# Filter network on 128 rows of half the times, projection weights loaded right behind x, filter tables and decay by GpSimd's queue, and idle transposes at the start

## The chip, the cores and the metric

The kernel runs on one core of one Trainium2 chip. The metric is the device time of one execution, in microseconds (us). Of the kernel before, three runs gave 1152.41, 1156.58 and 1158.32, so its median is 1156.58 us. All rows shown of it come from one more execution, which the hardware profiler recorded.

## The reference

The kernel computes one encoder layer on x of 1024 positions by 1024 channels in float32. Cut to what matters here:

```python
h = rms_norm(x, g_norm)
proj = h @ w_in                      # 1024 x 5280: hyena input, gates, latent q and kv, ...
# implicit filters of the long convolution, L = 1024 positions
z = concat([t, cos(ang), -sin(ang)])         # (L, 33), a constant table
f = sin(freq_1 * (z @ w_f1 + b_f1))          # (L, 64)
f = sin(freq_2 * (f @ w_f2 + b_f2))          # (L, 64)
k = (f @ w_f3).reshape(L, 2, 2, 512) * decay # order, direction, channel
k_spec = rfft(concat([k[:, :, 0], k[::-1, :, 1]]))   # filter spectra
u = short_conv(proj[...]); v, x1, x2 = split(u)
for o, gate in enumerate((x1, x2)):
    v = gate * (irfft(rfft(v, 2 * L) * k_spec[:, o])[:L] + v * hy_bias[o])
# beside it: latent attention of 8 heads; both branches are gated, merged, and w_out adds to x
```

## The kernel before, in words

A float32 product is made of three matmuls: each operand is split into a high part that ScalarE casts and a low part that VectorE subtracts (`split`, `gsplit`, `mm3`). The tiles are 128 partitions wide. A scheduler puts the instructions of each engine into one fixed order before the run, and each engine works through its own list in order. DMAs are issued from lists too: SP's and ScalarE's in this kernel; a DMA behind a waiting instruction on its list waits with it. Buffers come from pools; a tile in memory that another tile held waits until the last reader of that one is done.

The start runs like this. Eight tiles of x (`x`, 512 KB each) are loaded by SP and ScalarE in turn (`load_x`), and behind them on SP `sel`, `wf1`, `wf2`, the position table `z2` (`filter_loads`) and the first projection weights `wr` (`proj_block`, L559). `build_hT` works in two halves of four x tiles: squares with sums (ScalarE L216, VectorE L214), twelve small VectorE instructions that make the reciprocal root (`rsqrt`, L152 to L158), scaled rows `xs` (L223), transposes into PSUM (`ptx`, L230), and the split into `hh` (L142) and `hl` (L143). From these the projection is computed block by block: `proj_block` loads two `wr` of 256 KB, makes `wh` and `wl` of each, and issues 48 matmuls `pm` of 128x512 (L567). The first blocks are eight of the gates (`fill_g`); their results go out as `gT`.

The filter network (`filter_mlp`) has both directions of time on 128 partitions, the direction's 64 hidden rows above each other, and all 1024 positions in two chunks of 512. So each of its two layers has two chunks with three matmuls `pf`, a sine layer (VectorE L254 to L260 brings the argument into range, ScalarE L261 takes the sine) and a split. `filter_tables` loads `w_f3` and splits it into `w3h` and `w3l`, and loads the transform tables `ku` as `kur` and splits them into `kuh` and `kul`. `filter_spectra` then makes four spectra (two orders, two halves of the channels): per spectrum four `dec` tables of 512 KB by SP's queue (L342), matmuls `pk` (L348, L349), products `kk` (L350), sums `A` and `B`, small transforms on VectorE (`w`, `res`, `rh`, `rl`), matmuls `pu` with `kuh` and `kul` (L128), and copies `kt` that go to DRAM as `kd`.

Behind the spectra come the projection blocks for the convolution (`proj_vx`: transposes `ptt`, copies `tt`, DMAs `u` and `x`), the tables of the second transform (`load_gu`: DMAs `gur` on SP's list, L621, then `guh` and `gul`), and the convolutions themselves (`convs`): `U` is read back from DRAM, its transforms meet the spectra `kt`, and matmuls `pu` and `pi` with `guh` and `gul` follow. `gur` and `U` share the tag `UY` of the pool `uq`, which lies in memory that the filter's pool `fp` has given back. The rest (attention, output products) is the same text before and after.

## Time and profile before

| | before |
|---|---|
| median of three runs | 1156.58 us (1152.41 to 1158.32) |
| profiled execution | 1155.32 us, span 1153.4 us |
| TensorE (PE) busy | 1099.4 us, 95% of the span, 5525 matmuls |
| VectorE (DVE) busy | 893.0 us, 77% |
| ScalarE (ACT) busy | 589.4 us, 51% |
| GpSimd (POOL) busy | 107.3 us, 9%, no DMA |
| DMA | 150.27 MB, mean 130 GB/s |

Busy time is the sum over instructions of an engine; the matmuls' ends are modelled. PEclk in a table by windows is the clock that TensorE was granted, 1.00 for 2.4 GHz and 0.50 for 1.2 GHz. In a timeline a row gives the start, the duration, the engine (SPq and ACTq are the lists that issue DMAs), the source line, and in brackets how long the engine stood idle before it and what released it. "L12" is line 12 of the kernel before in every row below; in the kernel after, lines stand 7 to 16 further down.

### The profile page before, as it was taken

What the parts mean: (1) busy time and instruction counts of PE and PEld (TensorE: products, weight loads), DVE (VectorE), ACT (ScalarE), POOL (GpSimd) and SP (SyncE); (2) the same over time, 40 slices, a digit from 0 to 9 for tenths busy, and PEclk for the clock granted to TensorE, in tenths of its full rate; (3) what the DMA queues carried; (4) which work ended last, traced back from release to release, by engine and by line L of the source; (5) the groups of instructions that cost most, each with busy time, mean ns of one, the idle gap of its engine ahead of it and who ended that gap; (6) DMA issues with size and microseconds to landing.
All of it is one profiled execution on the core that took longest, in us unless ns stands there. A gap on an engine that the chain in (4) does not pass through costs nothing.

```text
span 1153.4 us, 15529 instructions
## 1 busy us (share of the span) xinstructions
PE 1099.4 (95%) x5525; PEld 909.7 (79%) x5525; DVE 893.0 (77%) x1631; ACT 589.4 (51%) x1101; POOL 107.3 (9%) x112
## 2 busy tenths in 40 slices
PE   4899999999999999999999999999999999999996
PEld 3678888888888888878887887787888887778874
DVE  6988788698788886778774893789788888478882
ACT  6745555754445434433433852777877776322420
POOL 0000000000000000000000132102200000250353
PEclk9989999999999999999999999899999999999998
DMA  5446444642335334334227557402202001896345
GB/s 212 133 146 198 155 163 174 205 119 65 89 91 147 105 115 128 91 88 127 91 83 233 148 154 248 146 29 74 92 25 77 1 20 50 274 298 217 91 128 182
DMA packets 119221, 150.27 MB, mean 130 GB/s; under 512 B 8548, under 2 KB 82408, under 8 KB 119144
## 3 DMA queue, kind: packets, MB, share of 16 engines
q1 hardware_dynamic: 107688, 120.97, 34.1%
q10 hardware_dynamic: 11456, 28.32, 6.6%
q8 instruction: 43, 0.70, 0.3%
q14 instruction: 34, 0.28, 0.1%
HBM read 101.81 MB, written 47.45 MB: 129 GB/s over the span
## 4 chain that ended last, share of the span: by engine, by line
PE 65%; DVE 14%; DMA 10%; ACT 6%; issue 3%; POOL 1%; SPq 0%; ACTq 0%; POOLq 0%; DVEq 0%
PE pm L567 33%; PE pu L128 8%; PE pt L903 4%; PE pi L128 4%; DMA wor<-in_w_out_dram 3%; PE S L119 2%; PE S L122 2%; PE S L121 2%; ACT pr L889 2%; PE pv L915 2%; PE pv L916 2%; DVE gg L988 1%; DMA out_dram<-xr 1%; DVE mo L139 1%; ACT PTh L138 1%
## 5 line engine op out<-in xcount | busy, mean ns | idle before, releaser
L567 PE MATMUL pm<-hh,wh 128*128 128x512 f32 x656 | 208.6, 393 | 1.8 <-DVE hl L143 0.9
L567 PE MATMUL pm<-hl,wh 128*128 128x512 f32 x656 | 208.9, 393 | 0.0
L567 PE MATMUL pm<-hh,wl 128*128 128x512 f32 x656 | 208.3, 392 | 0.1
L567 PEld LDWEIGHTS pm<-hh,wh 128*128 128x128 f32 x656 | 123.1, 189 | 27.7 <-DVE hl L143 1.1
L567 PEld LDWEIGHTS pm<-hh,wl 128*128 128x128 f32 x656 | 123.2, 188 | 26.0 <-DVE wl L139 0.5
L567 PEld LDWEIGHTS pm<-hl,wh 128*128 128x128 f32 x656 | 123.0, 188 | 25.3
L138 ACT CAST wh<-wr 128x512 fp32r<-128x512 f32 x98 | 60.3, 621 | 158.1 <-PE pm L567 107.7
L138 ACT CAST PTh<-pt 128x512 fp32r<-128x512 f32 x128 | 72.8, 587 | 41.1 <-PE pt L903 39.6
L139 DVE TENSOR_TENSOR PTl<-pt,PTh 128x512 fp32r<-128x512 f32 x128 | 83.8, 682 | 10.8 <-ACT PTh L138 10.2
L887 DVE TENSOR_REDUCE mx<-S 128x1 f32<-128x1024 f32 x64 | 77.9, 1217 | 13.2 <-PE S L122 13.1
L139 DVE TENSOR_TENSOR wl<-wr,wh 128x512 fp32r<-128x512 f32 x95 | 66.8, 708 | 15.7 <-ACT wh L138 15.4
L903 PE MATMUL pt<-ident,pr 128*128 128x128 f32 x512 | 75.9, 278 | 2.4 <-DVE PTl L139 1.4
L889 ACT ACTIVATE pr<-S,mx 128x1024 f32<-128x1024 f32 x64 | 71.8, 1121 | 7.0 <-DVE mx L887 6.6
L903 PEld LDWEIGHTS pt<-ident,pr 128*128 128x128 f32 x512 | 59.3, 142 | 18.2 <-DVE PTl L139 4.7
L915 PE MATMUL pv<-PTh,vc 128*128 128x256 f32 x256 | 69.1, 297 | 0.4 <-DVE at L926 0.4
L916 PE MATMUL pv<-PTl,vc 128*128 128x256 f32 x256 | 67.9, 293 | 0.0
L473 DVE TENSOR_TENSOR t<-pu,kt 128x512 f32<-128x512 f32 x64 | 41.0, 681 | 31.3 <-PE pu L128 30.7
L138 ACT CAST rh<-res 128x512 fp32r<-128x512 f32 x64 | 39.5, 619 | 41.8 <-PE pu L128 20.5
L119 PE MATMUL S<-kh,qh 96*128 96x512 f32 x128 | 54.5, 426 | 2.4 <-ACT pr L889 2.3
L121 PE MATMUL S<-kh,ql 96*128 96x512 f32 x128 | 53.5, 418 | 0.0
L122 PE MATMUL S<-kl,qh 96*128 96x512 f32 x128 | 52.5, 410 | 0.0
L915 PEld LDWEIGHTS pv<-PTh,vc 128*128 128x128 f32 x256 | 48.5, 189 | 4.7 <-DVE at L926 1.9
(285 smaller groups left out, 2391.2 us busy)
## 6 DMA issues: line engine op xcount, KB each, us to landing
wr<-in_w_in_dram SPq DMA_DIRECT2D x82, 256.0 KB, 3.2
wor<-in_w_out_dram SPq DMA_DIRECT2D x36, 256.0 KB, 4.7
dec<-in_dec_dram SPq DMA_DIRECT2D x16, 512.0 KB, 3.6
gT<-ob ACTq DMA_DIRECT2D x16, 512.0 KB, 2.9
gg<-gT SPq DMA_DIRECT2D x16, 512.0 KB, 4.4
kd<-kt ACTq DMA_DIRECT2D x28, 256.0 KB, 2.3
kt<-kd SPq DMA_DIRECT2D x28, 256.0 KB, 2.7
m<-gg ACTq DMA_DIRECT2D x16, 256.0 KB, 4.3
```

The lines of the kernel that those rows point to most:

```text
L119: m = nc.tensor.matmul(out, lhsT=lh, rhs=rh, start=start, stop=False)
L121: nc.tensor.matmul(out, lhsT=ll, rhs=rh, start=False, stop=False)
L122: nc.tensor.matmul(out, lhsT=lh, rhs=rl, start=False, stop=stop)
L128: m = self.nc.tensor.matmul(out, lhsT=x, rhs=y, start=n == 0, stop=n == len(ops) - 1)
L138: self.behind(self.nc.scalar.copy(out=hi, in_=x), after)
L139: (eng or self.nc.vector).tensor_tensor(out=lo, in0=x, in1=hi.bitcast(F32), op=ALU.subtract)
L567: nc.tensor.matmul(ps[c][0:m], lhsT=w[:, i, 0:m], rhs=h[d][:, c * 512:(c + 1) * 512], start=(d == 0 and f == 0), stop=(d == 7 and f == 2))
L887: nc.vector.tensor_reduce(out=mx, in_=ps, axis=AX.X, op=ALU.max, negate=True)
L889: i = nc.scalar.activation(out=pr, in_=ps, func=AF.Exp, bias=mx, accum_out=RS[h // 2][:, qb, h % 2:h % 2 + 1])
L903: nc.tensor.transpose(out=pt[:, i], in_=pr[:, kb * P:(kb + 1) * P], identity=self.ident)
L915: nc.tensor.matmul(pv, lhsT=V[h][:, kb], rhs=hi[:, kb], start=(kb == 0), stop=False)
L916: nc.tensor.matmul(pv, lhsT=V[h][:, kb], rhs=lo[:, kb], start=False, stop=(kb == 7))
```

## The change

The filter network now works on the first 512 positions in the upper 64 rows and on the last 512 in the lower 64, for one direction; the other direction is the same result read backwards. One chunk per layer is left, with three `pf` instead of six, and the second direction is made by two reversed casts on VectorE (`h[:, ::-1]`). The high and low parts of `z2` and `ku` come from the host as tables of their own, so no engine splits them. GpSimd issues the DMAs of `z2h` and `z2l` (256 KB each) once the seventh x tile is there, those of `kuh`, `kul` (1.18 MB each) and `sel` once `hh[7]` of the first half is there (`follow`), and all `dec` and `hy_bias` tables. `sel` and `z2` no longer stand before the first `wr` on SP's list. `w_f3` is loaded twice (four DMAs of 256 KB), so that its split needs two instructions of 128 rows per engine instead of half rows. 36 transposes of raw x tiles into a PSUM tile that nothing reads (`idle`) stand on TensorE before the first `ptx`. The gates' output is issued one block later (`gates`), and the second gate block's split is put behind `half0`, the last cast of the first half. The last step of the range reduction in a sine layer merges two constants into one (three L258 become two).

```diff
-    z2 = np.zeros((P, L), f32)
-    z2[:33] = z.T
-    z2[64:97] = z[::-1].T
+    z2 = np.zeros((P, L // 2), f32)
+    z2[:33] = z[:L // 2].T
+    z2[64:97] = z[L // 2:].T
...
+    t = {"sel": sel, "gu": gu, "dec": d2, "rt": rt, "ident": np.eye(P, dtype=f32)}
+    for n, x in (("z2", z2), ("ku", ku)):
+        t[n + "h"], t[n + "l"] = _parts(x)
+    return t
...
+        idle = self.pp.tile([P, 512], F32, tag="tp", bufs=2, name="idle")
+        for i in range(4):
+            for j in range(8 if i < 3 else 12):
+                nc.tensor.transpose(out=idle[:, :P], in_=xt[i][:, (j % 8) * P:(j % 8 + 1) * P], identity=self.ident)
...
-    def filter_loads(self, f1):
+    def filter_loads(self, fp, f1):
         nc, a = self.nc, self.a
-        self.selr = f1.tile([P, P], F32, tag="selr", name="selr")
-        nc.sync.dma_start(out=self.selr, in_=a["sel"])
         self.wf1 = f1.tile([P, P], F32, tag="wf1", name="wf1")
         nc.sync.dma_start(out=self.wf1, in_=a["wf1"])
         self.wf2 = f1.tile([P, P], F32, tag="wf2", name="wf2")
         nc.sync.dma_start(out=self.wf2, in_=a["wf2"])
-        self.z2 = f1.tile([P, L], F32, tag="z2", name="z2")
-        nc.sync.dma_start(out=self.z2, in_=a["z2"])
+        self.z2 = [f1.tile([P, L // 2], F32R, tag="z" + x, name="z" + x) for x in "hl"]
+        self.kuh = fp.tile([P, 18, P], F32R, tag="kuh", name="kuh")
+        self.kul = fp.tile([P, 18, P], F32R, tag="kul", name="kul")
+        self.sel = self.cp.tile([P, P], F32R, tag="sel", name="sel")
+        self.follow(f1, self.xt[6][0:1, 0:1], ((self.z2[0], a["z2h"]), (self.z2[1], a["z2l"])))
+
+    def follow(self, pool, x, moves):
+
+        nc = self.nc
+        dum = pool.tile([1, 1], F32, tag="fol", bufs=2, name=self.nm("fol"))
+        last = nc.gpsimd.tensor_copy(out=dum, in_=x)
+        for out, in_ in moves:
+            i = nc.gpsimd.dma_start(out=out, in_=in_)
+            self.behind(i, last)
+            last = i
 
     def filter_mlp(self, fp, f1):
+
         nc, a = self.nc, self.a
         self.w3h = [fp.tile([P, 2, HY], F32R, tag=f"w3h{d}", name=f"w3h{d}") for d in range(2)]
         self.w3l = [fp.tile([P, 2, HY], F32R, tag=f"w3l{d}", name=f"w3l{d}") for d in range(2)]
-        self.h2 = [fp.tile([P, L], F32R, tag=f"h2{d}", name=f"h2{d}") for d in range(2)]
-        z2, fv = self.z2, self.fv
-        zh = f1.tile([P, L], F32R, tag="zh", name="zh")
-        zl = f1.tile([P, L], F32R, tag="zl", name="zl")
+        self.h2 = {(d, c): fp.tile([P, L // 2], F32R, tag=f"h2{d}{c}", name=f"h2{d}{c}") for d in range(2) for c in range(2)}
+        fv, (zh, zl) = self.fv, self.z2
+        self.follow(f1, self.hh[7][0:1, 0:1].bitcast(F32), ((self.kuh, a["kuh"]), (self.kul, a["kul"]), (self.sel, a["sel"])))
+
+        wf3 = [f1.tile([P, 2, HY], F32, tag=f"wf3{d}", name=f"wf3{d}") for d in range(2)]
+        w3v = a["w_f3"][0].rearrange("k (o d c) -> d k o c", o=2, d=2)
+        for d in range(2):
+            for s in range(2):
+                self.behind(nc.scalar.dma_start(out=wf3[d][64 * s:64 * s + 64], in_=w3v[d]), self.half0)
         w1h = f1.tile([P, P], F32R, tag="w1h", name="w1h")
         w1l = f1.tile([P, P], F32R, tag="w1l", name="w1l")
         w2h = f1.tile([P, P], F32R, tag="w2h", name="w2h")
         w2l = f1.tile([P, P], F32R, tag="w2l", name="w2l")
         self.split(self.wf1, w1h, w1l, after=self.half0)
         self.split(self.wf2, w2h, w2l, after=self.half0)
-        h1h = f1.tile([P, L], F32R, tag="h1h", name="h1h")
-        h1l = f1.tile([P, L], F32R, tag="h1l", name="h1l")
+        h1h = f1.tile([P, L // 2], F32R, tag="zh", name="h1h")
+        h1l = f1.tile([P, L // 2], F32R, tag="zl", name="h1l")
+        ps = self.pp.tile([P, L // 2], F32, tag="cv", bufs=CVB, name=self.nm("pf"))
+        self.mm3(ps, w1h, w1l, zh, zl, True, True)
+        x = self.sin_layer(f1, ps, fv[:, 0:1], fv[:, 1:2], L // 2)
+        self.split(x, h1h, h1l)
+        for d in range(2):
+            self.split(wf3[d], self.w3h[d], self.w3l[d], after=self.half0)
+        ps = self.pp.tile([P, L // 2], F32, tag="cv", bufs=CVB, name=self.nm("pf"))
+        self.mm3(ps, w2h, w2l, h1h, h1l, True, True)
+        x = self.sin_layer(f1, ps, fv[:, 2:3], fv[:, 3:4], L // 2)
         for c in range(2):
...
+            a_, b_ = slice(64 * c, 64 * c + 64), slice(64 - 64 * c, 128 - 64 * c)
+            h, r = self.h2[0, c], self.h2[1, 1 - c]
+            nc.scalar.copy(out=h[a_], in_=x[a_])
+            nc.vector.tensor_tensor(out=h[b_], in0=x[a_], in1=h[a_].bitcast(F32), op=ALU.subtract)
+            nc.vector.tensor_copy(out=r, in_=h[:, ::-1].bitcast(F32))
...
-                nc.sync.dma_start(out=bia, in_=a["hy_bias"][:, o, cs])
+                nc.gpsimd.dma_start(out=bia, in_=a["hy_bias"][:, o, cs])
                 for tp in range(4):
                     dec = wk.tile([P, 2, 2, CW], F32, tag="dec", bufs=2, name=self.nm("dec"))
-                    nc.sync.dma_start(out=dec, in_=a["dec"][hf, tp].rearrange("p (d t c) -> p d t c", d=2, t=2))
+                    nc.gpsimd.dma_start(out=dec, in_=a["dec"][hf, tp].rearrange("p (d t c) -> p d t c", d=2, t=2))
...
+                            b = 2 * tp + i
+                            h = h2[d, b // 4][:, b % 4 * P:(b % 4 + 1) * P]
+                            nc.tensor.matmul(ps[:, i], lhsT=h, rhs=w3h[d][:, o, cs], start=True, stop=False)
+                            nc.tensor.matmul(ps[:, i], lhsT=h, rhs=w3l[d][:, o, cs], start=False, stop=True)
...
-    def proj_block(self, c0, m=P):
+    def proj_block(self, c0, m=P, after=None):
...
-            self.split(raw[:, :, 0:m], wh[:, :, 0:m], wl[:, :, 0:m])
+            self.split(raw[:, :, 0:m], wh[:, :, 0:m], wl[:, :, 0:m], after=after)
...
-    def fill_g(self, b):
+    def gates(self, bs):
+
+        ps = None
+        for b in bs:
+            new = self.proj_block(3232 + b * P, P, self.half0 if b == 1 else None)
+            if ps is not None:
+                self.gate_out(b - 1, ps)
+            ps = new
+        self.gate_out(bs[-1], ps)
+
+    def gate_out(self, b, ps):
         nc = self.nc
-        ps = self.proj_block(3232 + b * P, P)
...
-                with k.pool("fpb") as fb:
-                    k.filter_tables(fb)
-                    with k.pool("fwk") as wk:
-                        k.filter_spectra(wk)
-                        for b in range(GEARLY):
-                            k.fill_g(b)
+                with k.pool("fwk") as wk:
+                    k.filter_spectra(wk)
+                    k.gates(range(GEARLY))
```

Two places show how the order moves. The first is VectorE's list at the start. Before, the first reciprocal root (`rt_176`, `ry_175`) runs through to the scaled rows `xs`, and the low parts `wl` of the first projection weights stand in the second one (`rt_263`, `ry_262`):

```order
L156 TENSOR_TENSOR rt_176<-ry_175 128x4
L157 SCALAR_TENSOR_TENSOR rt_176<-rt_176,rv_174 128x4
L158 SCALAR_TENSOR_TENSOR ry_175<-rt_176,ry_175 128x4
L223 TENSOR_SCALAR xs_189<-x_115,ry_175 128x1024
...
L223 TENSOR_SCALAR xs_195<-x_121,ry_175 128x1024
L152 TENSOR_SCALAR rv_261<-ss 128x4
L153 TENSOR_SCALAR rt_263<-rv_261 128x4
L139 TENSOR_TENSOR wl_1569<-wr_1566,wh_1568 128x512
L154 TENSOR_SCALAR ry_262<-rt_263 128x4
L139 TENSOR_TENSOR wl_1599<-wr_1596,wh_1598 128x512
```

Now both `wl` stand inside the first one (`rt_218`, `ry_217`):

```order
L165 TENSOR_TENSOR rt_218<-ry_217 128x4
L148 TENSOR_TENSOR wl_1558<-wr_1555,wh_1557 128x512
L166 SCALAR_TENSOR_TENSOR rt_218<-rt_218,rv_216 128x4
...
L165 TENSOR_TENSOR rt_218<-ry_217 128x4
L148 TENSOR_TENSOR wl_1588<-wr_1585,wh_1587 128x512
L166 SCALAR_TENSOR_TENSOR rt_218<-rt_218,rv_216 128x4
L167 SCALAR_TENSOR_TENSOR ry_217<-rt_218,ry_217 128x4
L233 TENSOR_SCALAR xs_231<-x_115,ry_217 128x1024
```

So the scaled rows now stand behind two instructions that need the weights `wr_1555` and `wr_1585` and ScalarE's casts of them, and on ScalarE's list the second cast stands behind the square of x tile 4.

The second place is SP's list about the end of the spectra. Before, the two DMAs `gur` of the second transform's tables stand ahead of all four DMAs `u` that carry the first convolution's input to DRAM (the last two come from `tt_2263`); each `gur` waits for a `pk` matmul of the last spectrum, the last reader of the memory that it fills:

```order
L621 DMA gur_2454<-in_gu_dram 128x1408
L621 DMA gur_2458<-in_gu_dram 128x1408
...
L613 DMA u_0_2104<-tt_2177 512x1x128
L613 DMA u_1_2105<-tt_2177 512x1x128
L481 DMA kt_2490<-kd_0_8_571 128x768
L481 DMA kt_2537<-kd_0_12_592 128x512
...
L613 DMA u_0_2104<-tt_2263 512x1x128
L613 DMA u_1_2105<-tt_2263 512x1x128
L559 DMA wr_2956<-in_w_in_dram 128x4x128
L699 DMA U_2462<-u_0_2104 128x1024
L699 DMA U_2462<-u_1_2105 128x1024
```

Now they stand about the last two `u` DMAs (`tt_2251`), and the first of them waits for the last `pu` matmul with `kuh` of the last spectrum:

```order
L566 DMA wr_2386<-in_w_in_dram 128x4x128
L566 DMA wr_2873<-in_w_in_dram 128x4x128
L628 DMA gur_2442<-in_gu_dram 128x1408
L620 DMA u_0_2092<-tt_2251 512x1x128
L620 DMA u_1_2093<-tt_2251 512x1x128
L628 DMA gur_2446<-in_gu_dram 128x1408
L488 DMA kt_2478<-kd_0_8_560 128x768
L488 DMA kt_2525<-kd_0_12_581 128x512
L715 DMA U_2450<-u_0_2092 128x1024
L715 DMA U_2450<-u_1_2093 128x1024
```

So the tables `gur`, which have moved into memory that `kuh` and `kul` held, are asked for later in the work, and the DMAs `u` and `U` of the first convolution stand behind them.

## Rows read from the trace of the kernel before

**Rows 1.** Busy time and granted clock of stretches (start:end, length, busy of each engine; instructions)

```profile
core 0: us, PE busy (x) PEld busy (x) DVE busy (x) ACT busy (x) POOL busy (x), PEclk, DMA share, GB/s
53.00:58.00 5.00, 0.00 (x1) 0.00 (x0) 5.00 (x8) 4.48 (x7) 0.00 (x0) 0.99 0.40 160
58.00:65.00 7.00, 5.68 (x17) 4.67 (x18) 5.64 (x10) 3.80 (x6) 0.00 (x0) 0.52 0.44 140
65.00:83.00 18.00, 18.00 (x92) 15.30 (x91) 15.59 (x28) 5.60 (x10) 0.00 (x0) 1.00 0.57 180
100.00:600.00 500.00, 499.61 (x2345) 412.20 (x2344) 399.88 (x774) 232.86 (x460) 1.60 (x24) 1.00 0.40 124
```

**Rows 2.** Timeline of the start: reciprocal root, scaled rows, transposes, weights, first projection

```profile
12.55 0.17 DVE L152 TENSOR_SCALAR rv<-ss 128x4 f32<-128x4 f32 x1
...
12.89 1.06 ACT L216 ACTIVATE sq<-x 128x1024 f32<-128x1024 f32 x1 [0.36 <-DMA x<-in_x_dram]
...
14.93 2.74 DVE L223 TENSOR_SCALAR xs<-x,ry 128x1024 f32<-128x1024 f32 x4
...
15.74 5.52 PE L230 MATMUL ptx<-ident,xs 128*128 128x128 f32 x28 [8.60 <-DVE xs L223]
...
16.79 0.62 ACT L138 CAST wh<-wr 128x512 fp32r<-128x512 f32 x1 [0.47 <-DMA wr<-in_w_in_dram]
17.57 0.62 ACT L138 CAST wh<-wr 128x512 fp32r<-128x512 f32 x1 [0.16 <-DMA wr<-in_w_in_dram]
...
17.87 0.69 DVE L139 TENSOR_TENSOR wl<-wr,wh 128x512 fp32r<-128x512 f32 x1
...
21.36 4.70 DVE L143 SCALAR_TENSOR_TENSOR hl<-ptx,cols,hh 128x512 fp32r<-128x512 f32 x7 [0.48 <-ACT hh L142]
...
22.17 0.50 PE L567 MATMUL pm<-hh,wh 128*128 128x512 f32 x1 [0.91 <-DVE hl L143]
```

**Rows 3.** Timeline of the filter network and the first spectrum's start

```profile
43.60 1.21 DVE L322 TENSOR_TENSOR w3l<-wf,w3h 64x1024 fp32r<-64x1024 f32 x1
...
51.19 3.69 DVE L258 SCALAR_TENSOR_TENSOR sx<-sk,sx 128x512 f32<-128x512 f32 x6
...
58.86 0.58 PE L348 MATMUL pk<-w3h,h 128*128 128x256 f32 x1 [5.86 <-DVE h L306]
...
83.04 0.28 PE L128 MATMUL pu<-rh,kuh 128*128 128x256 f32 x1
```

**Rows 4.** Chain that ended last, from the spectra's end to the first convolution

```profile
209.81 2.75 PE pu L128 x12
212.56 8.21 PE pm L567 x36
220.76 0.45 PE ptt L611 x4
...
222.47 2.97 DMA u<-tt
...
225.50 5.00 DMA U<-u
...
244.05 1.43 PE pi L128 x12
```

**Rows 5.** The tables `gur` of the second transform (min/median/max in ns, first and last start)

```profile
L138 ACT CAST guh<-gur x2: 1378/1378/1378, 216.9 to 218.2; 128x1408 fp32r<-128x1408 f32 x2
L139 DVE TENSOR_TENSOR gul<-gur,guh x2: 1619/1620/1620, 219.6 to 221.2; 128x1408 fp32r<-128x1408 f32 x2
...
DMA to landing us min/median/max: 4.2/4.2/4.2
```

**Rows 6.** The page's table of DMA issues, the row of `dec`

```profile
dec<-in_dec_dram SPq DMA_DIRECT2D x16, 512.0 KB, 3.6
```

67 lines of the change are left out of this document (14 added, 53 removed).

## The prediction

> **What bounds the kernel now.** I read the table by windows first. From 65 us on TensorE is the bound: 18.00 of 18.00 us busy from 65 to 83, and 499.61 of 500 us from 100 to 600, with VectorE at four fifths [rows 1]. So up to 600 us a microsecond is worth something only where TensorE waits or runs slowly, and that is the start: 0.00 us busy from 53 to 58, and a granted clock of 0.52, the lower of its two levels, in the 7 us behind that idle stretch [rows 1]. Then I read the timeline of the start. The scaled rows `xs` begin at 14.93 us, the first projection matmul at 22.17 [rows 2], the first `pk` comes after 5.86 us of waiting for `h` from the filter network, and the first `pu` stands at 83.04 [rows 3]. Last I read the chain about the first convolution, because the changed order moves its tables [rows 4, 5].
>
> **What TensorE loses at the start.** Between 22.17 and 83.04, 60.9 us, its list holds 171 `pm`, 12 `pf`, 36 transposes and 32 `pk`. A `pm` takes 8.21/36 = 0.228 us, a 128x128 transpose 0.45/4 = 0.113, a 128x256 matmul 1.43/12 = 0.119 [rows 4]. That is 39.0 + 2.7 + 4.1 + 3.8 = 49.6 us, so 11.3 us go to waiting and the lower clock; 5.86 of them are the one wait for `h` [rows 3].
>
> **The change, part by part.**
>
> *Filter on half the times.* Six `pf` go: 6 x 0.228 = 1.4 us of TensorE. On VectorE a sine layer's long steps fall from six in 3.69 us for two chunks [rows 3] to two, some 1.2 us. Two of four sines, the splits of `z2` and `ku` on two engines, and half of the `h` steps go as well. Two reversed casts of 128x512 come in; no row has one, so I bound them by 0.3 us (half of a row below) and 1.4 (twice it) and take the 0.69 us of a `wl` [rows 2]. Shortening this chain pays through the 11.3 us: while it ran, TensorE had only two gate blocks (96 `pm`) ahead of the first `pk`; now its list has 129 there.
>
> *The weights in front.* Both `wl` now stand inside the first reciprocal root, so `xs` waits for two weight loads. Before, the casts of these weights began on landing, at 16.79 and 17.57 [rows 2], 0.78 us for 256 KB. The 512 KB of `z2` and the 64 KB of `sel` that stood ahead would be 1.8 us of that: the first weight lands at 15.0 at the earliest, and at 16.8 if GpSimd's `z2h` and `z2l`, the same bytes, share the engines. I take 16.0. Then come the cast 0.62, `wl` 0.69, six root steps of (14.93 - 12.55)/12 = 0.20 us [rows 2]; on ScalarE the second cast stands behind another square of x, 1.06 us [rows 2], and ends near 18.4. With the second `wl` and two steps `xs` starts at about 19.5, 4.6 us later than now (18.5 to 20.3 by the bounds).
>
> *The idle transposes* do not reach that far. They end soon after the fourth x tile, whose sum is used at 12.55 [rows 2]: 12 last ones at 0.2 are done by 15.0. Up to 20.3 TensorE is idle again for 5 us, as long as the stretch from 53 to 58, behind which the clock was low [rows 1]. So I count `ptx` at today's pace, 28 in 5.52 us [rows 2], and the first `pm` at 22.17 + 4.6 = 26.8. If the clock stays up, 28 x (0.197 - 0.113) = 2.4 us go there, but `hl` then waits for VectorE, and at most 1.3 us arrive.
>
> *New waits between 27 and 65 us.* VectorE's list now has `w1l`, `w2l`, the first range reduction step and two `w3l` (1.21 us each for as many columns [rows 3]) ahead of the second block's `wl`; the third block's load waits for that one. Nothing in the trace shows this wait. It is 1.0 us if the first block's matmuls cover most, and 4.6 if both `w3l` and the load follow one another uncovered. I take 2.8, the middle. `h` should be ready at about 63, which is when TensorE comes to `pk` by its own list (26.8 + 129 x 0.228 + 36 x 0.113 + 1.4 + waits), so the 5.86 us wait is gone, and what is late next is the weights.
>
> *Sum at the first `pu`.* 192 `pm`, 6 `pf`, 36 transposes, 32 `pk` are 53.1 us: 26.8 + 53.1 + 2.8 = 82.7. Before reaches the same work 21 `pm` later than 83.04, at 87.8. TensorE is 5.1 us ahead.
>
> *The tables of the second transform.* Here I expect most of that to be given back. `gur` now waits for the last `pu` of the spectra. Its place: up to it, 11 `pm` and 8 transposes more than before, 3.4 us, so 212.56 [rows 4] + 3.4 + 82.7 - 83.04 = 215.6. The last two `u` and both `U` stand behind it on SP's list. `gur` lands 4.2 us on, `guh` takes 1.4 and `gul` 1.6 [rows 5], then the first `U` may be issued, which takes 5.00 us: 227.8. Before, `U` landed at 230.50 and the first `pi` came at 244.05 [rows 4], 13.55 us later; now that would be 241.4. TensorE's own list holds 92 `pm`, 16 transposes and 12 small `pu` up to that `pi`, 24.2 us (before 31.5), and would be there at 239.8. So it waits 1.6 us at least by this count; 0 if part of those 13.55 us is TensorE's own work; 5.8 if the second `gur` and the two `kt` tables ahead of `U` cost another 4.2 us. I take 3.5.
>
> *`dec` and `hy_bias` by GpSimd.* I cost them at nothing: the first two tables land long before `pk`, and a later one has the time of seven VectorE instructions of 128x512, about 4.8 us, against 3.6 us of landing now [rows 6]. No GpSimd DMA is in this trace, so the landing is open; the bound is the rival below.
>
> **Sum.** 5.1 us ahead at the first `pu` (11.3 lost before and 1.4 of `pf`, against 4.6 and 2.8 of new delay, up to rounding) less 3.5 given back is 1.6: 1155.32 - 1.6 = 1153.7 us by the profiled execution. The median of the runs is 1.3 us above that execution; halfway, I say 1154.3 us. With the bounds (5.1 ahead is 2.5 to 7.5, the later wait 0 to 5.8) this case reaches from 1149 to 1158.5.
>
> **Rivals.**
>
> 1. *The gain is kept.* The weights land at 15.0, or the wait at the first `pi` is hidden, as TensorE has waited only 0.39 us in 500 so far [rows 1]. Then 5 to 7.5 us stay: 1148 to 1150.5. Against it speaks the list of SP, on which nothing can pass `gur`.
> 2. *The shorter network does not reach the end at all.* `xs` at 20.3, waits of 4.6 us, 2.5 ahead, and 3.5 to 5 lost at the tables: 1156 to 1159. For it speaks that one edit puts two DMAs into the root's chain.
> 3. *Slower: `dec` comes late.* If a table by GpSimd's list takes over 4.8 us, `kk` and with it the spectrum wait. At twice today's landing, 7.2 us [rows 6], it is 2.4 us late. The third and fourth table of a spectrum are asked for only once a buffer is free, so 4 x 2 x 2.4 = 19 us over the four spectra; less the 5.1 us ahead that is 1169 with nothing hidden, and with 5 us of it behind gate blocks some 1164. VectorE is busy 15.59 of 18 us there [rows 1], and the lists of GpSimd are otherwise short, so neither is excluded. The Trainium skill, "SBUF — State Buffer", section "SBUF: two separate sides", says that a DMA issued from GpSimd gets its descriptors written by GpSimd itself and starves while VectorE holds the shared port in its fast modes, and gives 3100 instead of 620 ns; by an estimate from these figures 2.5 us would be added, 6.1 in all, which is over the 4.8. Nothing in this trace shows it. The products and sums of the spectra are at the slow pace of 0.69 us for 512 columns, which is why this stays the smallest case.
>
> **How the numbers follow.** The forecast gets 0.53, the first rival 0.23, the second 0.13, the third 0.11. A measurement of this kernel can tell about 0.5%, 5.8 us, from no change: faster is below 1150.8, slower above 1162.4. Faster is the first rival and a little of the forecast, 0.24; slower the third, 0.11; between them 0.65. The range for 8 in 10 takes in the forecast's own range, the upper half of the first rival and the second: 1149 to 1161.
>
> **What would show it.** Right: `xs` at 19 to 20 us, the first `pm` near 27, no wait over 1 us at the first `pk`, the first `pu` near 83 with all of the fourth gate block done, and at about 240 a wait of 2 to 5 us before the first `pi`, with `gur` issued near 216. Wrong: `xs` before 17 (the weights came early), a granted clock of 1.00 and `ptx` at 0.11 us from the first one (the idle transposes hold it), no wait at 240 (then the time is near 1149), or `kk` waiting for `dec` in each spectrum (then it is above 1160).

## The result and the profile after

The changed kernel takes 1163.86 us, the median of 13 runs (1158.56 to 1167.63); the kernel before took 1156.58 us beside it, also of 13 runs (1151.88 to 1160.18). The ratio is 1.0066, with a 95% interval of 1.0051 to 1.0082: slower by 0.66%, 7.6 us, where 1154.3 us was forecast with a range of 1149 to 1161. The profiled execution of after took 1167.63 us (span 1165.8), 12.3 us more than that of before. That is more than the medians differ by, so the accounts below go by how much later TensorE comes to the same matmul than before, and not by the spans.

The table by windows of after, the stretches of [rows 1] and one ahead of them (start:end, length, busy of each engine; instructions):

```profile
core 0: us, PE busy (x) PEld busy (x) DVE busy (x) ACT busy (x) POOL busy (x), PEclk, DMA share, GB/s
45.00:53.00 8.00, 6.05 (x15) 4.62 (x16) 5.51 (x9) 6.12 (x8) 0.00 (x0) 0.57 0.43 124
53.00:58.00 5.00, 5.00 (x23) 4.13 (x22) 1.91 (x3) 2.82 (x5) 0.00 (x0) 1.00 0.49 137
58.00:65.00 7.00, 7.00 (x32) 5.79 (x31) 4.15 (x7) 3.77 (x4) 0.00 (x0) 1.00 0.38 95
...
100.00:600.00 500.00, 496.49 (x2318) 408.19 (x2317) 396.88 (x766) 232.87 (x462) 7.41 (x35) 1.00 0.40 123
```

The idle stretch from 53 to 58 of before is gone, and with it the low clock behind it. But both stand again in front of it: from 45 to 53 TensorE is busy for 6.05 of 8 us at a granted clock of 0.57. From 100 to 600 it now loses 3.5 us, where it lost 0.4.

The start came as forecast. Its timeline in after, beside [rows 2]:

```profile
16.10 0.69 DVE L148 TENSOR_TENSOR wl<-wr,wh 128x512 fp32r<-128x512 f32 x1 [2.54 <-ACT wh L147]
...
18.76 2.74 DVE L233 TENSOR_SCALAR xs<-x,ry 128x1024 f32<-128x1024 f32 x4
...
19.57 6.18 PE L240 MATMUL ptx<-ident,xs 128*128 128x128 f32 x28 [5.84 <-DVE xs L233]
...
26.09 0.50 PE L574 MATMUL pm<-hh,wh 128*128 128x512 f32 x1 [0.34 <-DVE hl L152]
```

VectorE sits 2.54 us in the middle of the reciprocal root, waiting for the first weight and its cast, and `xs` starts 3.83 us later than before.

What went wrong is between 40 and 70 us. Four rows of TensorE's timeline there (columns as in [rows 2]):

```profile
46.95 1.22 PE L574 MATMUL pm<-hh,wh 128*128 128x512 f32 x2 [3.05 <-ACT wh L147]
...
49.67 1.05 PE L574 MATMUL pm<-hh,wh 128*128 128x512 f32 x2
...
53.45 0.62 PE L574 MATMUL pm<-hh,wl 128*128 128x512 f32 x2
...
69.04 0.39 PE L355 MATMUL pk<-w3h,h 128*128 128x256 f32 x1
```

A wait of 3.05 us for a cast, then rows of two `pm` that last 1.05 us where 0.62 is usual, and the first `pk` at 69.04, 10.2 us later than before [rows 3]. TensorE doesn't wait at that `pk`, because gate blocks stand in front of it. ScalarE's timeline shows why `h` is late:

```profile
45.33 1.04 ACT L147 CAST w3h<-wf 128x1024 fp32r<-128x1024 f32 x1 [4.46 <-DMA wf<-in_w_f_dram]
...
51.50 0.62 ACT L147 CAST wh<-wr 128x512 fp32r<-128x512 f32 x1 [1.50 <-DMA wr<-in_w_in_dram]
52.14 1.28 ACT L271 ACT_TABLE_LOAD   x1
53.43 0.63 ACT L271 ACTIVATE sx<-sx 128x512 f32<-128x512 f32 x1
...
61.19 0.62 ACT L147 CAST wh<-wr 128x512 fp32r<-128x512 f32 x1 [4.55 <-PE pm L574]
61.83 1.28 ACT L699 ACT_TABLE_LOAD   x1
63.12 0.69 ACT L699 ACTIVATE ob<-pm,cols 128x512 f32<-128x512 f32 x1
63.83 1.28 ACT L271 ACT_TABLE_LOAD   x1
65.12 0.63 ACT L271 ACTIVATE sx<-sx 128x512 f32<-128x512 f32 x1
65.78 1.28 ACT L699 ACT_TABLE_LOAD   x1
67.07 0.69 ACT L699 ACTIVATE ob<-pm,cols 128x512 f32<-128x512 f32 x1
67.66 0.61 ACT L330 CAST h<-sx 64x512 fp32r<-64x512 f32 x1
```

ScalarE is idle for 4.46 us for the last part of `w_f3`. Then both sines and the casts `h1h` and `h` stand behind casts `wh` that wait for weights still on their way, or for a buffer that TensorE is still reading (4.55), and between gates `ob`, with a table load (`ACT_TABLE_LOAD`, 1.28 us) at each change of function. VectorE has the arguments of the sines ready at 51.30 and 61.86; the sines start at 53.43 and 65.12. VectorE's last step ahead of the second sine:

```profile
61.43 0.43 DVE L270 TENSOR_SCALAR sx<-sx 128x512 f32<-128x512 f32 x1
```

The chain of waits goes the same way (start, length, what; its last row belongs to the second transform, below):

```profile
36.60 8.66 DMA wf<-in_w_f_dram
...
46.95 10.06 PE pm L574 x31
...
222.88 4.81 DMA gur<-in_gu_dram
```

The page's row of `dec`, beside [rows 6], and TensorE's first `pi`:

```profile
dec<-in_dec_dram POOLq DMA_DIRECT2D x16, 512.0 KB, 4.6
```

```profile
248.96 0.39 PE L137 MATMUL pi<-ph,guh 128*128 128x256 f32 x1 [1.28 <-ACT ph L147]
```

`gur`, the tables of the second transform, is issued at 222.88, 7.3 us after the 215.6 of the forecast; 5.1 us of that are the later first `pu`. The first `pi` starts at 248.96 (before 243.9) after a wait of 1.28 us for ScalarE's cast `ph`. `dec` lands in 4.6 us at the median (before 3.6).

### The profile page after: what moved, and what is told of

It reads as the page before. It is cut to its first block, busy times and chain, and to the rows that moved or that the text cites. A ratio compares the mean times of both kernels' runs of the same rounds, so it can differ in the third digit from the quotient of the medians.

```text
span 1165.8 us, 15589 instructions
## 1 busy us (share of the span) xinstructions
PE 1105.7 (95%) x5555; PEld 913.0 (78%) x5555; DVE 882.4 (76%) x1610; ACT 580.0 (50%) x1089; POOL 120.4 (10%) x137
## 4 chain that ended last, share of the span: by engine, by line
PE 63%; DVE 13%; DMA 12%; ACT 7%; issue 3%; POOL 1%; SPq 0%; POOLq 0%; ACTq 0%; DVEq 0%
PE pm L574 29%; PE pu L137 7%; PE pt L919 4%; PE pi L137 4%; DMA wor<-in_w_out_dram 3%; PE S L128 2%; ACT pr L905 2%; PE S L130 2%; PE S L131 2%; PE pv L931 2%; PE pv L932 2%; PE pmo L130 1%; PE pmo L128 1%; DMA out_dram<-xr 1%; PE pmo L131 1%
## 5 line engine op out<-in xcount | busy, mean ns | idle before, releaser
L903 DVE TENSOR_REDUCE mx<-S 128x1 f32<-128x1024 f32 x64 | 77.9, 1217 | 12.8 <-PE S L131 12.6
```

The source lines that it names most:

```text
L903: nc.vector.tensor_reduce(out=mx, in_=ps, axis=AX.X, op=ALU.max, negate=True)
```

## The experiments

The same landmarks of the profiles that the argument uses (us; below zero is ahead of before). "First pu, same work" sets the first `pu` against before's 83.04 and takes off 0.228 us for each `pm` more that stands ahead of it: 171 in before, 192 in after and in `e1`, `e2`, `e9` and `e10`, 168 in `e12` to `e14`, 167 in `e17`. "Behind at 370" is how much later than before TensorE starts the same matmul, at 370 us.

| | ratio to before (95%) | first pk | first pu | first pi | first pu, same work | behind at 370 |
|---|---|---|---|---|---|---|
| before | | 58.9 | 83.0 | 243.9 | 0 | 0 |
| after | 1.0066 (1.0051 to 1.0082) | 69.0 | 87.8 | 249.0 | 0.0 | 5.90 |
| e1_tables_held | 1.0075 (1.0053 to 1.0098) | 69.7 | 88.6 | 250.0 | 0.7 | 5.73 |
| e2_gu_early | 1.0080 (1.0052 to 1.0108) | 68.4 | 87.2 | 252.4 | -0.6 | 8.19 |
| e9_gur_front | 1.0069 (1.0041 to 1.0097) | 67.4 | 86.2 | 247.4 | -1.7 | 10.12 |
| e10_bytes_early | 1.0046 (1.0029 to 1.0063) | 64.6 | 83.4 | 245.7 | -4.4 | 2.60 |
| e14_act_order | 1.0049 (1.0032 to 1.0066) | 62.5 | 81.3 | 248.4 | -1.0 | 4.18 |
| e12_h_early | 1.0002 (0.9991 to 1.0013) | 57.9 | 76.8 | 244.3 | -5.6 | 0.05 |
| e13_h_early_gu | 1.0012 (0.9998 to 1.0025) | 57.9 | 76.8 | 242.2 | -5.6 | -1.82 |
| e17_xs_early | 1.0037 (1.0022 to 1.0053) | 59.7 | 79.4 | 247.3 | -2.7 | 2.85 |

Each landmark is of one execution, and executions of one kernel differ (before: 1151.88 to 1160.18 us). `e16_seven_gates`, which has the start of `e13_h_early_gu`, came to its first `pk` at 60.0 instead of 57.9, so differences of 2 us in these columns say little.

**When the bytes are asked for.** From 20 to 30 us the DMA engines move 21 GB/s in after and from 30 to 40 us 278: GpSimd's `kuh`, `kul` and `sel` (2.4 MB) and `w_f3` (1 MB) run together, and the first two `dec` with them:

```profile
30.00:40.00 10.00, 9.26 (x54) 7.04 (x53) 8.31 (x13) 6.02 (x12) 4.50 (x8) 1.00 0.94 278
```

The first test holds GpSimd's tables until `w_f3` is there:

```diff
-        self.follow(f1, self.hh[7][0:1, 0:1].bitcast(F32), ((self.kuh, ...), (self.kul, ...), (self.sel, ...)))
+        self.follow(f1, wf3[1][64:65, 0, 0:1], ((self.kuh, ...), (self.kul, ...), (self.sel, ...)))
```

> The changed kernel with one edit: GpSimd asks for kuh, kul and sel only when the last w_f3 block has landed. Theory A (the fourth w_f3 block took 8.66 us because the 2.3 MB of tables shared the DMA engines with it, and that is where the gain of the start was lost): w_f3 lands within 4 to 5 us of its issue, near 41 us, no wait of TensorE at 47 us, a granted clock of 1.00 from 45 to 52, the first pu near 83.5 instead of 87.97, and the median 4 to 4.5 us lower, 1159.5. Rival B (the w_f3 block is late by its own queue, ScalarE's): it lands at 45 as now, the first pu stays at 88, the median stays at 1163.9. Rival C (the tables, asked for later, are now what the first pu waits for): w_f3 early, but a wait for kuh before the first pu, and the median within 1 us of 1163.9.

Measured: 1165.35 us, no gain. The wait for `w_f3` is gone (TensorE is busy for 9.09 us of 40 to 50), but the tables now press on the weights. Of its chain, and of its TensorE timeline:

```profile
44.55 7.17 DMA wr<-in_w_in_dram
```

```profile
55.43 0.79 PE L128 MATMUL pf<-h1h,w2h 128*128 128x512 f32 x1 [4.45 <-ACT h1h L147]
```

256 KB of weights take 7.17 us, and the same casts ahead of `h1h` wait for them. Moving the bytes back moved the wait. The second test asks for all of them earlier, in the empty stretch:

```diff
+            self.xs0 = getattr(self, "xs0", xs[0])
...
-        self.follow(f1, self.hh[7][0:1, 0:1].bitcast(F32), (kuh, kul, sel))
...
-                self.behind(nc.scalar.dma_start(out=wf3[d][64 * s:64 * s + 64], in_=w3v[d]), self.half0)
+        self.follow(f1, self.xs0[0:1, 0:1], [(wf3[d][64 * s:64 * s + 64], w3v[d]) ...] + [kuh, kul, sel])
```

> The changed kernel with w_f3 and then kuh, kul and sel asked for by GpSimd behind the first xs, near 19 us, where the DMA engines moved 21 GB/s between 20 and 30 us, instead of behind hh near 30 (the tables) and on ScalarE's list at 36.6 (the fourth w_f3). Theory A (the start is bound by the bytes that are asked for between 30 and 45 us: what is delayed is w_f3 in the changed kernel and the weights wr in e1, so only a shift into the idle stretch helps): no wait of TensorE over 1 us between 30 and 60 us, h at 60 to 62, the first pu near 83.5 instead of 87.97, the median 4 to 4.5 us lower, 1159.5. Rival B (not bytes but ScalarE's and VectorE's lists of the filter network bound the first pk): no DMA wait is left but the first pk still comes after 69, and the median is within 1 us of 1163.9. Rival C (the tables now delay the weights of the second block at 20 to 30 us): a wait for wr or wl before 45 us, gain under 2 us.

Measured: 1162.18 us, and the first `pu` at 83.41, as expected, 4.4 us earlier than in after. The time is not as expected: the ratio is 0.20% lower, 2.3 us, with overlapping intervals. From 20 to 30 us 279 GB/s move, and TensorE's wait of 3.05 us is gone. But ScalarE's list still holds `h` up: a cast `wh` in front of the first sine waits for its load, and one in front of the second for TensorE:

```profile
47.78 0.62 ACT L147 CAST wh<-wr 128x512 fp32r<-128x512 f32 x1 [1.81 <-DMA wr<-in_w_in_dram]
...
56.79 0.62 ACT L147 CAST wh<-wr 128x512 fp32r<-128x512 f32 x1 [4.02 <-PE pm L572]
```

**The order on ScalarE's list.** Now the casts of the third block's weights go behind `h1h`, those of the fourth behind `h`, and the second block's gate behind `h` as well; everything else stays as in the run before:

```diff
-        self.split(x, h1h, h1l)
+        self.h1i = nc.scalar.copy(out=h1h, in_=x)
+        nc.vector.tensor_tensor(out=h1l, ...)
...
-            nc.scalar.copy(out=h[a_], in_=x[a_])
+            self.hi = nc.scalar.copy(out=h[a_], in_=x[a_])
...
-            new = self.proj_block(3232 + b * P, P, self.half0 if b == 1 else None)
+            new = self.proj_block(3232 + b * P, P, {1: self.half0, 2: self.h1i, 3: self.hi}.get(b))
...
+            if b == 1:
+                self.behind(i, self.hi)     # i: the activation that makes ob
```

> e10 with one more edit on ScalarE's list: the casts of the third and fourth block's weights stand behind h1h and h, and the second block's gate behind h, so that neither a wait for wr (45.74 to 51.04 us in e10) nor two extra loads of the activation table (57.43 and 61.37, 1.28 us each) stand ahead of the two sines. Theory A2 (formed from e1 to e11: the four spectra follow each other at 37 to 40 us each at VectorE's pace, so it is the first pk, which waits for h, that sets the last pu and the first pi; 58.9, 212.2 and 243.9 us before the change, 69.0, 222.4 and 249.0 in the changed kernel, 64.6, 218.7 and 245.7 in e10): first pk at 57 to 59, last pu at 212 to 215, first pi at 241 to 244, the median 3 to 5 us under e10's 1162.2, so 1158. Rival B2 (TensorE's own list, not h, sets the end: it is busy all the time from 53 us on in e10, so h can come as early as it likes): first pk early, the first pi not before 245, the median within 1 us of 1162.2.

Measured: 1156.20 us, ratio 1.0002, and 0.6% under the changed kernel: the whole loss is gone, with intervals that lie apart. Of the 11.1 us by which the first `pu` is earlier than in after, 5.5 are 24 `pm` that now stand behind it; 5.6 us are a lead on before in the same work. ScalarE's timeline, to be held against that of after:

```profile
47.62 0.63 ACT L272 ACTIVATE sx<-sx 128x512 f32<-128x512 f32 x1
...
55.83 0.63 ACT L272 ACTIVATE sx<-sx 128x512 f32<-128x512 f32 x1 [4.29 <-DVE sx L271]
56.50 1.26 ACT L329 CAST h<-sx 64x512 fp32r<-64x512 f32 x2
57.78 1.28 ACT L698 ACT_TABLE_LOAD   x1
```

The sine now waits for VectorE's argument, `h` follows it at once, and between the first sine and `h` no table load is left, where three stood. TensorE is busy for 10.00 of 10 us from 45 to 55 and from 55 to 65. The same edit of the order alone, on the changed kernel with its late bytes:

> The changed kernel with the order edit of e12 on ScalarE's list alone; w_f3 and the tables are asked for where the changed kernel asks for them. It tells the two parts of e12 apart. Theory A2 (both parts are needed: the late w_f3 holds the list until 45.3 us, the order costs what comes behind it): w_f3 lands at 45 as in the changed kernel, then one table load, sine, h1h, second sine; h 4 to 6 us earlier than 70.5, first pk at 63 to 65, and the median 3 to 4 us under the changed kernel, 1160. Rival (the order alone is the cause, and the late w_f3 was hidden all along): first pk at 58 to 60 and a median of 1156 to 1157 as in e12. Rival (the transfers alone): first pk at 69, 1163 to 1165.

Measured: 1161.18 us, ratio 1.0049, first `pk` at 62.5. By the ratios the early bytes alone give 0.20% and the order alone 0.17%, and the interval of each overlaps that of after; both together give 0.64%, clear of it. That each obstacle left alone still holds the network up is read from the landmarks: the first `pk` at 64.6 and 62.5, and at 57.9 without both.

**The second transform's tables.** The forecast put its loss at 240 us on `gur`. First the memory is laid out so that `gur` no longer waits for the last `pu` (the weights of the third filter layer are taken ahead of `kuh`):

```diff
+        self.w3h = [...]; self.w3l = [...]; self.h2 = {...}     # moved up, ahead of kuh
         self.kuh = fp.tile([P, 18, P], F32R, tag="kuh", name="kuh")
```

> The changed kernel with one edit: w3h, w3l and h2 are allocated ahead of kuh and kul, so the tables gur of the second transform go into memory whose last reader is the last pk and not the last pu. No instruction changes its place. Theory A (4.4 us between 209 and 273 us were lost because gur had to wait for the last pu): gur is issued near 216 instead of 222.88, no wait over 0.5 us before the first pi, and the median 3.5 to 4.4 us lower, 1160. Rival B (it is the place of gur on SP's list, behind two u and two weight loads, that makes it late): issued at 220 or later, and the median at most 1 us lower.

Measured: 1163.95 us, no gain, and the first `pi` is later, at 252.4. SP's list:

```profile
218.97 0.46 SPq L628 DMA_DIRECT2D gur<-in_gu_dram  x1
222.49 5.71 SPq L620 DMA_DIRECT2D u<-tt  x2
```

`gur` is issued 3.9 us earlier than in after, but the two `u` behind it take until 228.2 to be issued. Then `load_gu` goes ahead of `proj_vx(0)` in the program too, with one weight load behind it:

```diff
-                k.proj_vx(0)
                 k.load_gu(gp)
+                k.proj_vx(0)
...
+            if c0 == 5 * P and g == 1:
+                self.behind(i, self.gur)
```

> The changed kernel with the tables gur of the second transform both in memory whose last reader is the last pk (as in e2) and put ahead of the second pair of u and of the last weight load on SP's list. Theory A (the 4.4 us between 209 and 273 us come from the place of gur in SP's list together with the memory that it waits for): gur issued near 198 us instead of 222.88, VectorE does not wait for gul, the first pi below 247 instead of 248.96, no stretch at the lower clock at 250, TensorE at most 1.5 us behind the kernel before at 273 us instead of 5.0, and the median 3.5 to 4.5 us lower, 1160. Rival B (it is VectorE's own list, which has come later and denser to this place, that sets the first pi; gur only stood in its shadow): gur early, the first pi still after 248, and the median within 1 us of the changed kernel's 1163.9.

Measured: 1164.53 us, ratio 1.0069, as after, although `gur` is issued at 198.0, 25 us earlier. The edit moved more than `gur`: 580 `pm` stand ahead of the first `pi` instead of 608, so TensorE is busy for only 29.7 of the 36 us from 209 to 245 (after 35.0), and the 28 `pm` come back as filler later (153.8 of 160 us busy from 600 to 760, after 147.8). Of the 10.12 us of the table 6.4 are these 28 (at 0.228). VectorE still waits for `guh`, and TensorE for VectorE:

```profile
227.35 1.63 DVE L148 TENSOR_TENSOR gul<-gur,guh 128x1408 fp32r<-128x1408 f32 x1 [7.60 <-ACT guh L147]
```

```profile
244.41 1.53 PE L620 MATMUL ptt<-ident,acc 128*128 128x128 f32 x8 [3.41 <-DVE acc L609]
```

ScalarE casts `guh` at 225.9, where its list has it, not when `gur` lands (4.2 us after its issue). So the transfer was not what ended last there, and the first `pi`, at 247.4, again waits 1.50 us for ScalarE's `ph`. Two more runs join this memory edit to the better starts:

> The edits of e9 and e10 together. Theory A (start and second transform are two separate losses against the gain that the change should have had): 8 us under the changed kernel, a median near 1156, level with the kernel before. Rival B (whatever is saved at one place is waited for at the next, since another engine than TensorE sets the pace up to 273 us): at most 3 us lower, 1161 or more.

> e12 with the memory of e2 (gur waits for the last pk and not for the last pu). In e12 and here gur stands on SP's list ahead of the second pair of u, not behind it as in the changed kernel. Theory A2: with the spectra early there is less filler behind them, so now gur's wait for the last pu shows: gur issued near 195 instead of 213, first pi 1 to 3 us earlier than in e12, median 1156 to 1157. Rival: gur loads beside kd and u and holds them up, as e2 had it (kd 7.29 us), and the time is within 1 us of e12's.

`e11_both` (both edits of `e9_gur_front`, on `e10_bytes_early`) took 1159.85 us, ratio 1.0036 (1.0021 to 1.0050), a little under `e10_bytes_early` though the intervals overlap; `e13_h_early_gu` (`e12_h_early` with the memory of `e2_gu_early`) 1157.47 us, ratio 1.0012, no faster than `e12_h_early`.

**`dec` by GpSimd.** Both DMAs go back to SP's list:

```diff
-                nc.gpsimd.dma_start(out=bia, in_=a["hy_bias"][:, o, cs])
+                nc.sync.dma_start(out=bia, in_=a["hy_bias"][:, o, cs])
...
-                    nc.gpsimd.dma_start(out=dec, in_=a["dec"][hf, tp]...)
+                    nc.sync.dma_start(out=dec, in_=a["dec"][hf, tp]...)
```

> The changed kernel with one edit: dec and hy_bias are asked for by SP's list again, as before the change. Theory A (dec by GpSimd costs next to nothing): the median within 1.5 us of 1163.9. Rival B (dec by GpSimd is late, 4.6 us of landing at the median against 3.6 before, and VectorE waits 3.3 us for it): VectorE's waits for dec gone, TensorE busy 120 of 120 us between 100 and 220 instead of 118.6, and the median 2 to 5 us lower.

Measured: 1165.31 us, ratio 1.0074 (1.0050 to 1.0097), the same as after. VectorE's waits for `dec` fall from 3.3 us to 0.7 without any gain. The landing is the same by either list:

```profile
dec<-in_dec_dram SPq DMA_DIRECT2D x16, 512.0 KB, 4.6
```

So GpSimd's queue is neither the cause of the loss nor of the 1.0 us by which `dec` lands later than before.

**The lead-in to `xs`.** Both `wl` of the first block go behind the first `xs` (`self.behind(wl, xs0)`):

> The changed kernel with one edit: on VectorE both wl of the first projection block stand behind the xs of the first group, as before the change. Theory A (two weight loads inside the root cost 4 us at the start): xs begins near 15 instead of 18.76, the first pm near 22 instead of 26.09, and since the tables are asked for as much earlier, all that follows shifts too: the first pu near 84, the median 4 us lower, 1160. Rival B (the start is bound by bytes: x, weights, w_f3 and tables come through the same DMA engines, and w_f3 lands near 45 whatever xs does): the first pm near 22 but the first pu still near 87 and the median within 1 us of 1163.9. By the way: with 2 us instead of 6 between the idle transposes and ptx the granted clock may stay at 1.00 there; then 28 ptx take about 4 us instead of 6.2.

Measured: 1165.07 us, ratio 1.0084 (1.0059 to 1.0109), no gain. Of its timeline:

```profile
15.87 3.27 PE L241 MATMUL ptx<-ident,xs 128*128 128x128 f32 x28 [1.75 <-DVE xs L233]
...
23.99 0.79 PE L575 MATMUL pm<-hh,wh 128*128 128x512 f32 x1 [4.85 <-DVE hl L152]
```

`xs` and `ptx` are 3.7 us earlier and `ptx` twice as fast, but `hh` stands behind the squares of the second group on ScalarE and begins at 20.80. TensorE waits 4.85 us, has the low clock after that (0.50 from 24 to 28), and the lead of the first `pm` is down to 2.1 us. So on `e13_h_early_gu` the same edit was run with the last two squares moved behind the casts `hh` of the first half:

> e13 with the edit of e4 (both wl of the first block behind the first xs) and, what e4 lacked, the last two squares of the second x group behind the first hh on ScalarE's list (in e4 four squares stood ahead of hh, which began at 20.80 instead of about 18.7, and a second idle stretch of 4.85 us followed). Theory: xs at 15, ptx at a clock of 1.00 in 3.3 us, first pm at 20 to 22 instead of 25.9, first pk at 54 to 56 instead of 57.9, last pu 2 to 4 us earlier than 206.1, first pi 2 to 4 us earlier than 242.2, and the median 2 to 4 us under e13's 1157.5: 1154 to 1155. Rival (the second x group now comes late): a wait for ptx of the second group before 40 us takes it back, the first pk at 57 or later, the time within 1 us.

Measured: 1158.54 us, ratio 1.0037. The first `pm` comes at 20.88, 5.2 us earlier than in after, but the squares are then missing for the second group's `xs`:

```profile
35.11 3.86 PE L248 MATMUL ptx<-ident,xs 128*128 128x128 f32 x16 [8.01 <-DVE xs L239]
```

**The idle transposes** are left out (four lines, `idle`), nothing else:

> The changed kernel without its 36 idle transposes. Theory: TensorE is idle for 5.84 us between them and ptx, the granted clock is 0.50 from 18.1 to 24.9 us all the same, so they do nothing: ptx in 6 us, first pm within 0.5 us of 26.09 and the median within 1.5 us of 1163.9. Rival (they do help the clock of what follows, as in e4, where 1.75 us lay between them and ptx and 28 ptx took 3.27 us at a clock of 1.00): ptx slower than 6.2 us, the median 1 to 3 us higher. Rival 2 (before the change there were none, and ptx ran 28 in 5.52 us at a clock of 1.00 after 8.6 idle us): the lower clock in the changed kernel at 18.1 comes from the idle transposes themselves; then the clock stays at 1.00 here and ptx take 5.5 us.

Measured: 1162.27 us, ratio 1.0052 (1.0032 to 1.0071); its interval overlaps that of after, so the idle transposes are shown neither to help nor to hurt. `ptx` starts at 19.75 there, beside 19.57. The expectation took before's `ptx` to have run at a clock of 1.00; that 1.00 is no record (see the last section).

**How many gate blocks stand beside the spectra.** In `e12_h_early` the lead of 5.6 us at the first `pu` is gone at 370. TensorE waits for `acc` of the convolution's projection on the way, 2.99 us at 228 and 1.12 at 242:

```profile
228.15 1.07 PE L617 MATMUL ptt<-ident,acc 128*128 128x128 f32 x8 [2.99 <-DVE acc L606]
```

The first of these waits goes back to ScalarE's list. The copy `sraw` that `acc` is made of starts at 222.89, behind two casts `guh` that wait for `gur` (1.96 and 1.78 us) and a cast `wh` that waits 1.44 us for its weight. The chain has this weight as

```profile
212.28 9.18 DMA wr<-in_w_in_dram
```

256 KB in 9.18 us, beside both `gur` (issued at 208.36 and 209.75, 0.72 MB each), two `kt` and two `u`; from 208 to 216 us the 16 DMA engines are busy all the time (a share of 1.0). In before the weight in this place lands in 4.51 us, and `guh` waits for nothing: `gur` was issued at 185 there. In `e13_h_early_gu` the weight takes 8.71 us and TensorE waits 2.52. So it looks like the start over again, bytes asked for together and casts that wait for them ahead of others on ScalarE's list; no run takes this apart.

Gate blocks fill such waits. Two runs on `e13_h_early_gu` change their number (`GEARLY = 8` to 9 and to 7; the rest come later):

> e13 with a ninth gate block in front of the first convolution instead of behind it (the number of early gate blocks 9 instead of 8, the same work in all). Theory A2: in e12 and e13 TensorE is 5.5 us ahead of the kernel before from 86 to 209 us and gives 3.5 to 4 us of it back between 209 and 245, because it has come to the first convolution before VectorE's chain has and has no other work there (waits of 2.99 and 1.12 us for acc in e12). 48 pm more, 10.9 us, fill that: no waits there, TensorE 5 us ahead still at 370 us, median 1151 to 1153, under the kernel before. Rival: the ninth block stands in TensorE's list ahead of the pu and pi that VectorE waits for, the chain moves back by as much, and the time stays within 1 us of e13's 1157.5.

> e13 with seven gate blocks in front of the first convolution instead of eight: the counterpart of e15. In e15 the waits between 209 and 245 us went (0.82 us idle instead of 2.52) and 8.2 us of idle time came back between 650 and 760 (15.68 instead of 7.49), where the block was missing as filler. Theory: filler is conserved. One block fewer in front puts 10.9 us more between 650 and 760, idle there 0 to 2 us instead of 7.5, and the projection blocks of the first convolution come 10.9 us earlier; but the spectra, at VectorE's pace, then leave TensorE idle before the first pi by 5 to 11 us more. Sum within 4 us of e13's 1157.5, either side. Rival (the first pi was late only because its projection blocks stand behind eight gate blocks): the first pi comes at 236 to 238 instead of 242.2, TensorE loses under 3 us before 245, and the median is 1152 or less, under the kernel before.

Measured: nine give 1163.01 us, ratio 1.0055 (1.0038 to 1.0071); seven 1157.66, 1.0024 (1.0010 to 1.0038); eight had 1.0012. The windows of eight, of nine and of seven, in this order:

```profile
209.00:245.00 36.00, 33.48 (x165) 28.22 (x164) 27.22 (x41) 19.27 (x31) 0.40 (x6) 0.95 0.57 181
...
650.00:760.00 110.00, 102.51 (x529) 86.14 (x528) 80.53 (x198) 62.95 (x119) 26.60 (x23) 0.95 0.52 166
```

```profile
209.00:245.00 36.00, 35.18 (x169) 28.80 (x170) 22.55 (x31) 20.23 (x33) 0.46 (x6) 1.00 0.47 140
...
650.00:760.00 110.00, 94.32 (x477) 78.82 (x477) 79.08 (x206) 61.90 (x118) 26.54 (x23) 0.92 0.52 167
```

```profile
100.00:209.00 109.00, 102.65 (x486) 82.50 (x485) 94.25 (x186) 54.27 (x115) 6.21 (x17) 0.97 0.45 148
...
650.00:760.00 110.00, 106.50 (x526) 88.65 (x525) 75.84 (x193) 60.00 (x113) 26.66 (x23) 0.97 0.55 177
```

With nine the wait at 209 to 245 shrinks (36 - 35.18 = 0.8 us idle instead of 2.5), and 15.7 us are idle at 650 to 760 instead of 7.5. With seven only 3.5 are idle there, but 6.35 at 100 to 209. A gate block spent in one place is missing in another; none of the three is best everywhere. Nine is slower than eight; seven and eight are not told apart, as their intervals overlap.

## Why the prediction was wrong, step by step

The step that failed is "New waits between 27 and 65 us", with its 2.8 us (1.0 to 4.6). From the first `pm` at 26.09 to the first `pu` at 87.81 lie 61.7 us, with 53.1 us of matmuls by the prediction's count: 8.6 us were lost. Of these 3.05 are the wait for a cast, 0.7 two small waits, and 3.0 the low clock behind it (31 `pm` in 10.06 us, against 31 x 0.228); the other 1.9 are in pieces too small to place. What the forecast lacked is named in the second and third points below: ScalarE's list, and the bytes that are asked for between 30 and 45 us. With both mended (`e12_h_early`) the first `pu` has the forecast's lead, 5.6 us against 5.1.

- *`xs` and the first `pm`*: right. 18.76 and 26.09 us, against 19.5 and 26.8. That the idle transposes do not reach `ptx` was right too: 28 in 6.18 us.
- *The wait for `h` is gone, and what is late next is the weights*: right in kind, and wrong in what it does. `h` was forecast at about 63. VectorE's part was in time: the second sine's argument was ready at 61.86. The prediction followed VectorE's list and TensorE's, and not ScalarE's, where the sines and `h` stand behind casts of weights and behind gates. The casts of `h` started at 67.66 and 68.29.
- *The DMAs*: the prediction counted the bytes of the first two weights at the start, but not those between 30 and 45 us, where 3.4 MB of tables and `w_f3` come at once, and 1 MB of `dec` with them. 256 KB of `w_f3` took 8.66 us. The Trainium skill, "DMA: Bandwidth & Descriptors", section "Issuing engines are not separate DMA queues", says that DMAs started by ScalarE, SyncE or GpSimd run on the same 16 engines and interleave. The runs agree: GpSimd's tables slowed `w_f3` on ScalarE's list in after, and `wr` on SP's list in `e1_tables_held`.
- *Sum at the first `pu`*: 82.7 forecast, 87.81 measured; before does the same work by 87.8. The lead of 5.1 us is 0. These are 5.1 of the 9.2 us between the forecast change (1.6 faster) and the measured one (7.6 slower); the next point has 2.4 more.
- *3.5 us given back about the second transform*: the place was right, the size too small, and the cause is not what the forecast had. After falls back by 5.9 us between the first `pu` and 370 us, and `e12_h_early`, which has the lead, by 5.7. In the forecast `gur` is what ends last. But a `gur` issued 25 us earlier (`e9_gur_front`, which moves other work too) leaves the first `pi` waiting and the time as it was. In after TensorE's waits there are 0.6 us for a `kk`, 0.85 for `acc` and 1.56 at the first `pi` for ScalarE's `ph` and VectorE's `pl`, and behind these the clock is 0.50 from 250.9 to 254.3, some 1.7 us more; in `e12_h_early` 4.1 us are waits for `acc`. In after 32 `pm` more than before stand ahead of the last `pu` of the spectra (516, before 484), so less filler is left behind it; but in `e12_h_early` there are as many as before (481), and it falls back as far. What holds `acc` up there, by the trace, are casts on ScalarE's list that wait for `gur` and for a weight beside it; this is argued, not shown. That gate blocks move such waits is shown by the runs with seven and nine.
- *`dec` by GpSimd at nothing* [rows 6]: right. It lands in 4.6 us at the median, just under the 4.8 that were allowed (up to 13.2 for single tables, and VectorE waits 3.3 us in all), and giving it back to SP changes nothing. The slower rival, which had this as its mechanism, is out; that the time it named (some 1164) came about by another is luck. The Trainium skill's rule in "SBUF — State Buffer", section "SBUF: two separate sides", gave 2.5 us more by the prediction's estimate. No run here shows such a delay: SP's landing in `e8_dec_sp` is 4.6 us too.
- *The rivals* "the gain is kept" and "the shorter network does not reach the end" are both wrong as they stood. The second had the right place, the start, but its largest loss there was 4.6 us, and 8.6 came.

Four table loads (1.28 us each) stand between 52 and 67 us in after, because gates and sines alternate. The Trainium skill, "ScalarE: Activation LUTs", section "What ACT_TABLE_LOAD costs", gives about 1.28 us for the load and 2.66 for a whole switch with its drain. These traces show the load (61.83 to 63.12, where the next function starts) and no drain beside it: the load starts 0.02 us after the instruction ahead of it ends.

What stays open: of the 7.6 us by the ratio, 5.90 stand at 370 us; the other 1.7 are not placed, since single executions differ by more than that. And with the start mended the kernel is level with before, not 1.6 us ahead: what takes the lead back about the first convolution is read from traces alone.

## What to carry to other kernels

When a chain is shortened, walk down the whole list of every engine that it passes through, and ask of each instruction in front of the chain's own what that one waits for: here late bytes and, in front of two sines, casts of weights and gates together cost as much as the chain had saved. Ask the same of transfers: bytes that are needed at 45 us should be asked for in the empty stretch at 20 us, and bytes moved behind them only press on the next load. Take both obstacles away together before judging either, and don't expect one engine's lead to last: at the next stage it waits for what the others bring, here `acc` and `ph`.

## What was not expected of the hardware

- A table by windows prints a PEclk of 1.00 also where the trace has no record of the clock. In `e7_no_idle` the first record begins at 24.52 us, in before at 20.38. Up to there `ptx` comes every 0.213 us, and from there on every 0.11. After has the pace of 0.213 at a recorded 0.50 (18.74 to 25.57), `e4_wl_behind` that of 0.11 at a recorded 1.00. Of after, and then of `e7_no_idle` on both sides of its first record (TensorE alone):

```profile
21.00:23.00 2.00, 2.00 (x11) 0.50 0.00 0
```

```profile
21.00:24.50 3.50, 3.50 (x18) 1.00 0.01 3
24.50:25.30 0.80, 0.80 (x7) 1.00 0.00 0
```

  So the pace of `ptx` follows the clock, and before's 28 in 5.52 us after 8.60 idle us [rows 2] were mostly at the lower level.
- The idle transposes do bring the clock up (in after the record of 1.00 begins at 11.92 us, in their midst). Behind them TensorE waits 5.84 us, the clock falls at 18.74, and all 28 `ptx` run at 0.50: 6.18 us. In `e4_wl_behind` the wait is 1.75 us, the clock stays, and 28 take 3.27 us.
- In after a wait of 3.05 us was followed by the low clock (0.57 on the mean from 45 to 53 us), which cost 3.0 us, as much as the wait itself.
- The landing of a transfer depends on its company far more than on its queue: the four DMAs of `w_f3` took from 3.8 to 12.8 us for the same 256 KB, and `dec` took 4.6 us at the median by GpSimd's list and by SP's.
